# A decoder trunk on one core: the values are projected before the index queries, and four smaller moves go with it

## The chip, the core and the metric

The kernel runs on one core of a Trainium2 chip. The metric is the device time of one execution in microseconds (us). The core has TensorE for matrix products (PE in the profile, with its weight loads as PEld), VectorE (DVE), ScalarE (ACT), GpSimd (POOL) and SyncE (SP), which here only issues DMAs. DMAs are issued from the queues of SP, ACT and POOL.

## The reference, cut to what matters

The trunk is one layer with 512 tokens and 2048 channels. Everything is float32. What the change touches:

```python
mod = silu(c) @ w_ada + b_ada                     # six rows of 2048: sh1, sc1, gt1, sh2, sc2, gt2
h = rmsnorm(x, g_mix) * (1 + sc1) + sh1
proj = h @ w_in                                   # q_a k_a v_a q_b k_b v_b qi ki wi g_a g_b
y_a = stick_breaking_attention(q_a, k_a, v_a) @ w_a
y_b = dsa_attention(rope(q_b), rope(k_b), v_b, rope(qi), rope(ki), wi) @ w_b
x = x + (1 + gt1) * ((sigmoid(g_a) * y_a + sigmoid(g_b) * y_b) @ w_o)
h = rmsnorm(x, g_ffn) * (1 + sc2) + sh2
u = h @ w_up;  u = conv_b + width-3 causal convolution of u over tokens
x = x + (1 + gt2) * ((silu(u[:, :5632]) * u[:, 5632:]) @ w_down)
return rmsnorm(x, g_final)
```

`qi` are the 1024 columns of the index queries, `v_a` the 1024 columns of the stick-breaking values. A fact that both versions use: with `amp = (1 + sc1) * g_mix` and `r = 1/rms(x)` of a token, `h @ w = r * ((x * amp) @ w) + sh1 @ w`. So a projection can start on `h0 = x * amp` before the norm is known; the product is then scaled by `r`, and a row `sh1 @ w`, the same for every token, is added. That row is called the shift row below.

## The kernel before

**Products.** Each float32 product is made of three fast ones: an operand is split into a high part (`hi`, `wh`: ACT copies it to a shorter format) and a low part (`lo`, `wl`: DVE subtracts), and `mm3` (L178 to L180) adds hi*hi, hi*lo and lo*hi in PSUM. `prep` loads a 128x1024 tile of weights (`raw`, 8 buffers, loaded by SP) and `parts` (L168 on ACT, L170 on DVE) splits it into one of three pairs of rooms `wh`, `wl`. PSUM has eight banks: `acc` (3), `att` (4), `outs` (1).

**adaLN.** `mod` is made on DVE: `ada_half` (L320, L321) loads 512 KB of `w_ada` and one DVE instruction multiplies it by a spread copy of `silu(c)` and sums it. There are two spread copies, `cb[0]` and `cb[1]`, for the first and the second 1024 channels, and each stays in a `raw` buffer, so that six are left for loads. 96 such halves (`ada_left`) are spread over later stages by `some_ada`.

**Stage 1, index queries (L396 to L427).** For each of the 16 tiles of 128 channels: two adaLN halves give `sc1` of the tile, `h0` is formed, and seven of the eight index query tiles are accumulated in seven PSUM banks. After the last tile the norm (`rms`, L368 to L379) is spread to all partitions.

**Stage 2, values (L459 to L480).** `h` is formed (L437 on DVE, L438 and L466 on ACT, L468 on DVE), its shift `sh1` by two more adaLN halves per tile, and the eight value tiles are accumulated in eight banks. Then come the small `tail` product, the eighth index query tile (`w_qi7`) and the first two query and key tiles.

**Stage 3, 31 units (L675 to L685).** `unit` makes two output tiles with one Strassen step: seven products of 8x3 matmuls of 128x256, whose weights DVE adds and subtracts (L268, L272, L306, L310) before they are split. At two places of each unit `between` takes one step of a list of tasks (`beside`): `rope_tables`, `shift_queries`, `index_ropes`, and then adaLN halves. `shift_queries` reads `w_qi` transposed and makes the shift row of the index queries by 28 DVE instructions; `index_ropes` scales a query tile by the norm (L647), adds the shift (L648, ACT) and rotates it (L616 to L624). At the second place a unit also makes one adaLN half.

**Stage 4, attention and output projection.** For each of 8 stick-breaking heads and 8 sparse heads DVE makes adaLN halves beside the attention, two per head in the first loop and four in the second; the indexer's top-128 search (MAX8, MATCH_REPLACE8, L779 and L780) runs on DVE beside the sticks.

**Stage 5, up-projection.** Six up tiles (`ups`, NU = 3 pairs) are made plainly while the second norm is applied; they stay in SBUF and are convolved by `finish` (L1123 to L1133) beside the first three units of the up-projection (j = 3, 4, 5), each of which also finishes its own pair. `yd` takes the results.

The order on each engine is that of the program as a scheduling layer arranges it from the code's order and `issue_after` pins (`behind`). The engines take their queues in order.

Of the kernel before, what the change touches and what calls it, by code (L numbers as in the profile page):

```python
# [35 lines left out]
NQ = 7  # L36
# [40 lines left out]
def block_kernel(ctx: ExitStack, tc: tile.TileContext, A: dict, out: bass.AP):  # L77
# [279 lines left out]
    cb = c_spread()  # L357
    nc.scalar.dma_start(c_col, A["c_col"])
# [3 lines left out]
    def rms(squares, blocks=range(NQB), bank=outs):  # L362
# [14 lines left out]
        yield  # L377
        out = bank()
        mm(out[:, at], ones, wide[:, at], start=True, stop=True)  # L379
# [4 lines left out]
    qi_ps = [acc() for _ in range(3)] + [att() for _ in range(4)]  # L384
    norm = None
# [10 lines left out]

    for k in range(KT):
        if k == 6:
            past = t2k("w", 2)[:, :P]
            with behind(pins["load"]):  # L400
                nc.sync.dma_start(const, A["consts"][:, :5])
                nc.sync.dma_start(past, A["consts"][:, 5])
            nc.gpsimd.tensor_copy(mask[0], ident)
            nc.gpsimd.tensor_copy(mask[1], past)
# [6 lines left out]
        if k == KT - 1:  # L411
            norm = rms([total])
            next(norm)
        ada_end(t, t + 1)
        stt(amp[:, 0, k : k + 1], mod[:, t : t + 1], 1.0, g_mix[:, k : k + 1], ALU.add, ALU.mult)
        h0 = slot(F32R), slot(F32R)
        act(h0[0], x, AF.Copy, scale=amp[:, 0, k : k + 1])
        stt(h0[1], x, amp[:, 0, k : k + 1], h0[0].bitcast(F32), ALU.mult, ALU.subtract)  # L418
        w = prep(A["w_qi"][k], NQ * P)
        for j in range(NQ):  # L420
            mm3(qi_ps[j], cols(w, j), h0, k == 0, k == KT - 1)
            if k == KT - 1 and j == 0:
                rstd = t2k("T", 2)
                act(rstd, next(norm), AF.Copy)
# [3 lines left out]


    dram = lambda name, n, w=S: [dr.tile([P, w], F32, tag=f"{name}{i}", name=f"{name}{i}") for i in range(n)]  # L430
    save = nc.gpsimd.dma_start
    qid, hd_, vd, rd = dram("qid", 8), dram("hd", KT // 2), dram("vd", 8), dram("rd", 1)[0]
    save(rd, rstd)
# [8 lines left out]
    def evac(ps, rows=slice(0, P)):  # L442
        o = slot()
        act(o[rows], ps[rows], AF.Copy)
        return o

    EARLY = (9,)
# [7 lines left out]
    pv = None  # L455

    def ada_tile(k):
        last = [ada_half(cb, k, half) for half in range(2)][1]
        ada_end(k, k + 1)  # L459
        return last  # L460

    ada_tile(0)
    for k in range(KT):
        modulate(xt[k], k, 0, xt[k])
        hi, lo = slot(F32R), slot(F32R)
        act(hi, xt[k], AF.Copy)  # L466
        with behind(*([ada_tile(k + 1)] if k + 1 < KT else [])):
            tt(lo, xt[k], hi.bitcast(F32), ALU.subtract)  # L468
        h.append((hi, lo))
        w = prep(A["w_va"][k])  # L470
        if k == 0:
            for j in range(NQ):
                save(qid[j], evac(qi_ps[j]))
            pv = [outs()] + [acc() for _ in range(3)] + [att() for _ in range(4)]
        if k % 2 == 0:
            save(hd_[k // 2], xt[k])
        for i in range(8):
            mm3(pv[i], cols(h[k], i % 4), cols(w, i // 4, S), k == 0, k == KT - 1)
        if k in EARLY:
            forms_late(EARLY.index(k))  # L480
    for i in range(8):
        save(vd[i], evac(pv[i]))
# [15 lines left out]
    for j, (src, dst) in enumerate(((A["w_qi7"], qid[7]), (A["w_x0"][0], xd[0]), (A["w_x0"][1], xd[1]))):  # L498
        ps = (acc, att)[j % 2]()
        for c in range(2):  # L500
            w = prep(src[c])
            for k in range(8):
                i = 8 * c + k
                last = mm3(ps, cols(w, k), h[i], i == 0, i == KT - 1)
                if j == 2 and k % 2:
# [81 lines left out]
    corr = macc[:, : 2 * NQ, :].rearrange("p (j a) b -> p j (a b)", a=2)  # L587

    def shift_queries():

        rows = [t2k(tag, 2) for tag in ("w", "T") for _ in range(2)]
        diag = None
        for i in range(5):
            if i:
                ps = outs()
                mm(ps, ones, diag, start=True, stop=True)
                act(rows[i - 1], ps, AF.Copy)
            if i < 4:
# [1020 lines left out]
```

## Time and profile before

| what | value |
|---|---|
| median of 3 runs | 2746.66 us (2745.15 to 2747.31) |
| the profiled execution's own time | 2744.77 us |
| its span, first to last instruction | 2742.9 us |
| busy: PE, DVE, ACT, POOL | 98%, 88%, 53%, 11% of the span |
| stage 1 (first product to the spread norm) | 13.5 to 98 us |
| stage 2, with the tail and the small tiles | 101.6 to some 239 us |
| stage 3 | some 239 to 830 us |
| attention | some 865 to 1180 us |
| first units of the up-projection | some 1500 to 1560 us |

In a row of a timeline stand the start, the busy time, engine, line, operation, out<-in and shape, and in brackets the idle time in front and what ended it. In a row of windows stand for each engine the busy time in the stretch and the number of instructions, the granted clock of PE, the share of the DMA engines and GB/s. A busy PE is modelled, so beside its busy time the number of matmuls is used: it shows what was really done in a stretch.

### The profile page before, as it was taken

What the parts mean: (1) busy time and instruction counts of PE and PEld (TensorE: products, weight loads), DVE (VectorE), ACT (ScalarE), POOL (GpSimd) and SP (SyncE); (2) the same over time, 40 slices, a digit from 0 to 9 for tenths busy, and PEclk for the clock granted to TensorE, in tenths of its full rate; (3) what the DMA queues carried; (4) which work ended last, traced back from release to release, by engine and by line L of the source; (5) the groups of instructions that cost most, each with busy time, mean ns of one, the idle gap of its engine ahead of it and who ended that gap; (6) DMA issues with size and microseconds to landing.
All of it is one profiled execution on the core that took longest, in us unless ns stands there. A gap on an engine that the chain in (4) does not pass through costs nothing. (4 is left out here: it accounts for less than half of the span.)

```text
span 2742.9 us, 47708 instructions
## 1 busy us (share of the span) xinstructions
PE 2678.6 (98%) x18704; PEld 2449.0 (89%) x18704; DVE 2409.0 (88%) x3452; ACT 1450.6 (53%) x2045; POOL 314.2 (11%) x519
## 2 busy tenths in 40 slices
PE   8999999999999999999999999999999999999996
PEld 6779999999998777889999999999999998888875
DVE  8978989988897899788888999999999997888876
ACT  4444454455556665434466555555555455546452
POOL 0010000001002011111220100000000001012112
PEclk9999999999999999999999999999999999999998
DMA  9973456755566458866773566666665436559686
GB/s 339 363 258 123 163 177 207 234 178 185 173 209 222 137 190 279 270 222 190 229 254 114 173 185 177 182 181 178 183 177 166 137 123 234 169 158 257 192 243 188
DMA packets 164189, 550.08 MB, mean 201 GB/s; under 512 B 21414, under 2 KB 21798, under 8 KB 163964
## 3 DMA queue, kind: packets, MB, share of 16 engines
q1 hardware_dynamic: 116220, 405.34, 44.7%
q0 software_dynamic: 47152, 141.30, 18.4%
q8 instruction: 147, 2.41, 0.3%
q14 instruction: 78, 0.64, 0.1%
q10 hardware_dynamic: 592, 0.39, 0.0%
HBM read 453.71 MB, written 89.83 MB: 198 GB/s over the span
## 5 line engine op out<-in xcount | busy, mean ns | idle before, releaser
L168 ACT ACTIVATE wh<-raw 128x1024 fp32r<-128x1024 f32 (+2 forms) x792 | 828.1, 1053 | 942.4 <-DVE raw L272 180.0
L170 DVE TENSOR_TENSOR wl<-raw,wh 128x1024 fp32r<-128x1024 f32 (+2 forms) x792 | 953.3, 1211 | 123.4 <-ACT wh L168 115.4
L178 PE MATMUL acc<-F,wh 128*128 128x256 f32 (+1 forms) x2464 | 706.9, 289 | 15.2 <-ACT wh L168 10.7
L180 PE MATMUL acc<-F,wl 128*128 128x256 f32 (+1 forms) x2464 | 706.8, 287 | 5.4 <-DVE wl L170 5.4
L179 PE MATMUL acc<-F,wh 128*128 128x256 f32 (+1 forms) x2464 | 707.4, 287 | 0.0
L178 PE MATMUL att<-F,wh 128*128 128x256 f32 (+1 forms) x2448 | 700.1, 288 | 5.2 <-DVE sp L308 4.2
L180 PE MATMUL att<-F,wl 128*128 128x256 f32 (+1 forms) x2448 | 700.5, 286 | 2.1 <-DVE wl L170 2.1
L179 PE MATMUL att<-F,wh 128*128 128x256 f32 (+1 forms) x2448 | 701.1, 286 | 1.2 <-DVE F L199 1.2
L178 PEld LDWEIGHTS acc<-F,wh 128*128 128x128 f32 x2464 | 462.4, 188 | 33.0 <-ACT wh L168 15.2
L180 PEld LDWEIGHTS acc<-F,wl 128*128 128x128 f32 x2464 | 462.7, 188 | 16.4 <-DVE wl L170 6.8
L178 PEld LDWEIGHTS att<-F,wh 128*128 128x128 f32 x2448 | 459.7, 188 | 18.0 <-issue 5.6
L179 PEld LDWEIGHTS acc<-F,wh 128*128 128x128 f32 x2464 | 463.1, 188 | 11.0 <-DVE F L418 0.9
L179 PEld LDWEIGHTS att<-F,wh 128*128 128x128 f32 x2448 | 459.7, 188 | 12.7 <-DVE F L199 4.3
L180 PEld LDWEIGHTS att<-F,wl 128*128 128x128 f32 x2448 | 459.6, 188 | 11.0 <-DVE wl L170 2.9
L321 DVE SCALAR_TENSOR_TENSOR raw<-raw,raw 128x1024 f32<-128x1024 f32 x155 | 185.7, 1218 | 0.0
L178 PE MATMUL att<-wh,F 128*128 128x512 f32 x448 | 178.3, 398 | 0.2 <-ACT wh L168 0.2
L179 PE MATMUL att<-wl,F 128*128 128x512 f32 x448 | 174.8, 390 | 0.0
L180 PE MATMUL att<-wh,F 128*128 128x512 f32 x448 | 174.8, 391 | 0.0
L268 DVE TENSOR_TENSOR raw<-raw,raw 128x1024 f32<-128x1024 f32 x80 | 97.5, 1218 | 39.6 <-DMA raw<-in_w_x 22.3
L179 PE MATMUL acc<-wl,F 128*128 128x512 f32 x288 | 113.8, 395 | 4.4 <-DVE wl L170 4.4
L178 PE MATMUL acc<-wh,F 128*128 128x512 f32 x288 | 112.5, 393 | 1.1 <-ACT wh L168 0.9
L180 PE MATMUL acc<-wh,F 128*128 128x512 f32 x288 | 112.8, 392 | 0.0
(360 smaller groups left out, 3620.7 us busy)
## 6 DMA issues: line engine op xcount, KB each, us to landing
raw<-in_w_up SPq DMA_DIRECT2D x164, 512.0 KB, 3.6
raw<-in_w_ada SPq DMA_DIRECT2D x155, 512.0 KB, 5.4
raw<-in_w_x SPq DMA_DIRECT2D x128, 512.0 KB, 4.3
raw<-in_w_down SPq DMA_DIRECT2D x104, 512.0 KB, 5.0
xd<-F POOLq DMA_DIRECT2D x64, 256.0 KB, 2.8
F<-xd POOLq DMA_DIRECT2D x64, 256.0 KB, 5.0
raw<-in_w_o SPq DMA_DIRECT2D x32, 512.0 KB, 5.3
soft<-in_w_gate SPq DMA_DIRECT2D x32, 512.0 KB, 4.1
```

The costliest lines, as they stand in the source:

```text
L168: pins["wh"] = act(wh, raw, AF.Copy)
L170: pins["wl"] = tt(wl, raw, wh.bitcast(F32), ALU.subtract)
L178: mm(ps, ah, bh, start=first, stop=False, skip_group_check=not check)
L179: mm(ps, ah, bl, start=False, stop=False, skip_group_check=not check)
L180: return mm(ps, al, bh, start=False, stop=last, skip_group_check=not check)
L268: last_v = tt(s, a21, a22, ALU.add)
L321: return stt(raw, raw, 1.0, cb[half], ALU.mult, ALU.mult, accum_out=macc[:, t, half : half + 1])
```

## The change

Five things are done.

1. **Values first.** Stage 1 now accumulates the eight value tiles from `h0`; the last two of the 16 tiles are reordered around the norm, so that four value tiles are still being summed behind the product that spreads the norm. Stage 2 accumulates all eight index query tiles (NQ = 8) from the finished `h`, so `w_qi7`, the scaling by the norm and the saved norm row `rd` go. The value tiles are scaled by `r` on their way out of PSUM (ACT) and saved beside stage 2.
2. **The values' shift row** `sh1 @ w_va` is made by `shift_values`: POOL loads `w_va` again, ACT scales it by `sh1` per partition, POOL adds up (`gpsimd.tensor_tensor`), two matmuls with ones sum over partitions, and eight accumulating DMAs add the row to the saved values. `shift_queries` goes. The order of tasks is now rope tables, a pause of two steps, index ropes, `shift_values`.
3. **adaLN by first halves.** `ada_left` takes all first halves, then all second halves. So `cb[1]` is given up after stage 2 (a copy waits in DRAM, `c_half`) and comes back when the second halves start; until then seven `raw` buffers serve loads. From the start of `shift_values` on each unit makes two adaLN halves instead of one, and heads 5 to 7 of the first attention loop and parts of heads 0 and 1 of the second make none.
4. **Index ropes** fetch the next tile one step ahead.
5. **Plain up tiles late.** `ups` are saved to DRAM, and `finish_first` fetches and finishes them in 21 single steps, one in each unit from j = 9 on.

```diff
-    qi_ps = [acc() for _ in range(3)] + [att() for _ in range(4)]
+    pv = [outs()] + [acc() for _ in range(3)] + [att() for _ in range(4)]
...
-        w = prep(A["w_qi"][k], NQ * P)
-        for j in range(NQ):
-            mm3(qi_ps[j], cols(w, j), h0, k == 0, k == KT - 1)
+        wv.append(prep(A["w_va"][k]))
+        if k < KT - 2:
+            for i in range(8):
+                value(i, k)
...
+    ada_tile(0)
+    for i in range(1, 4):
+        value(i, KT - 2)
+    for k in range(KT - 2, KT):
+        value(0, k)
+    v0 = evac(pv[0])
+    norm = rms([total])
+    r_col = next(norm)
+    for i in range(4, 8):
+        value(i, KT - 2)
+    w_next = prep(A["w_qi"][0])
+    for i in range(1, 4):
+        value(i, KT - 1)
+    spread = next(norm)
+    act(rstd, spread, AF.Copy)
+    with behind(pins["spread"]):
+        for i in range(4, 8):
+            value(i, KT - 1)
...
-    def shift_queries():
...
+    def shift_values():
+        total = [t2k("T", 2) for _ in range(2)]
+        def weights(k):
+            w = sb.tile([P, 1024], F32, tag="soft", name=nm("soft"))
+            save(w, A["w_va"][k])
+            return [w[:, i * S : (i + 1) * S] for i in range(2)]
+        w = weights(0)
+        light.append(1)
+        yield
+        for k in range(KT):
+            for i in range(2):
+                act(w[i] if k else total[i], w[i], AF.Copy, scale=mod[:, k : k + 1])
+                if k:
+                    nc.gpsimd.tensor_tensor(total[i], total[i], w[i], ALU.add)
+            if k + 1 < KT:
+                w = weights(k + 1)
+            yield
...
-    ada_left = [(t, half) for t in range(32, 80) for half in range(2)]
+    ada_left = [(t, half) for half in range(2) for t in range(32, 80)]
+    cb[1] = None
...
-                if i:
+                if i or light:
                     some_ada()
...
-            some_ada(2)
+            some_ada(2 if hd < 5 else 0)
...
-            some_ada(2)
+            some_ada(2 if hd > 1 else 0)
...
-            some_ada(2)
+            some_ada(2 if hd else 0)
...
-    ups = [evac(ps) for ps in ups]
+    ud = dram("ud", 2 * NU)
+    for i, ps in enumerate(ups):
+        save(ud[i], evac(ps))
...
-        if j < 2 * NU:
-            finish(j - NU, *ups[2 * (j - NU) : 2 * (j - NU) + 2])
-        elif j < 2 * NU + 2:
+        if 2 * NU <= j < 2 * NU + 2:
...
+        if j >= 3 * NU:
+            run(first_tiles)
         finish(j, *unit(A["w_up"][j - NU], f, beside_up))
```

How the order of instructions moves at the places that matter. First PE at the border of stages 1 and 2. Before, L379 spreads the norm; of the last tile two products follow it, and then the first value product (`outs<-wh,F`), which needs the finished `h`:

```order
L180 MATMUL att_109<-F_771,wl_70 128x512
L178 MATMUL att_110<-F_771,wh_67 128x512
L379 MATMUL outs_783<-T_764,const 128x512
L179 MATMUL att_110<-F_772,wh_67 128x512
L180 MATMUL att_110<-F_771,wl_70 128x512
L178 MATMUL outs_876<-wh_73,F_840 128x512
```

Between the sums of squares (L368) and L379 stood 19 products. In the changed kernel L370 sums the squares and L381 spreads the norm:

```order
L180 MATMUL acc_108<-wh_67,F_779 128x512
L370 MATMUL outs_810<-const,T_122 128x1 x4
L178 MATMUL acc_109<-wh_67,F_778 128x512
L179 MATMUL acc_109<-wl_70,F_778 128x512
L180 MATMUL acc_109<-wh_67,F_779 128x512
L381 MATMUL outs_849<-T_818,const 128x512
L178 MATMUL att_110<-wh_67,F_778 128x512
```

Three products stand between the two now, and twelve (`att_110` to `att_113`) between L381 and the first product that needs `h`.

Second DVE in a unit of stage 3, from L310 to L268, the sum of two loaded tiles of the next unit. Before, in a unit with a step of `index_ropes` (L647):

```order
L170 TENSOR_TENSOR wl_70<-raw_7486,wh_67 128x1024
L170 TENSOR_TENSOR wl_76<-raw_7456,wh_73 128x1024
L310 TENSOR_TENSOR raw_7456<-raw_7456,raw_7486 128x1024
L170 TENSOR_TENSOR wl_83<-raw_7450,wh_79 128x1024
L276 TENSOR_TENSOR sp_7548<-att_7448,ta_7484 128x256
L647 TENSOR_TENSOR w_7518<-w_7518,w_5773 128x512
L321 SCALAR_TENSOR_TENSOR raw_7581,macc_68<-raw_7581,raw_92 128x1024
L170 TENSOR_TENSOR wl_70<-raw_7456,wh_67 128x1024
L268 TENSOR_TENSOR raw_7711<-raw_7677,raw_7679 128x1024
```

With six buffers the tile `raw_7679`, the second input of L268, takes the room of `raw_7450`, which the fourth row (`wl_83`) reads last. Now, in a unit beside `shift_values`:

```order
L310 TENSOR_TENSOR raw_6554<-raw_6554,raw_6584 128x1024
L170 TENSOR_TENSOR wl_83<-raw_6548,wh_79 128x1024
L276 TENSOR_TENSOR sp_6649<-att_6546,ta_6582 128x256
L321 SCALAR_TENSOR_TENSOR raw_6686,macc_68<-raw_6686,raw_92 128x1024
L170 TENSOR_TENSOR wl_70<-raw_6554,wh_67 128x1024
L268 TENSOR_TENSOR raw_6816<-raw_6782,raw_6784 128x1024
L170 TENSOR_TENSOR wl_76<-raw_6552,wh_73 128x1024
L308 TENSOR_TENSOR sp_6649<-att_6546,ta_6582 128x256
L321 SCALAR_TENSOR_TENSOR raw_6851,macc_68<-raw_6851,raw_92 128x1024
```

No task has a DVE instruction here any more, the unit has two adaLN halves (L321), and the later of the two loads waits for the room of `raw_6584`, which L310 reads last: four instructions ahead of L268, where in units beside the index ropes more stand between.

Third POOL in the same units. Before, its queue held only DMAs there. Now (L728 saves a unit's results, L623 loads `w_va`):

```order
L623 DMA soft_6220<-in_w_va 128x1024
L728 DMA xd_1771<-F_6215 128x512
L728 DMA xd_1772<-F_6216 128x512
L633 ISA
L633 TENSOR_TENSOR T_6153<-T_6153,soft_6220 128x512
L633 TENSOR_TENSOR T_6154<-T_6154,soft_6220 128x512
L623 DMA soft_6385<-in_w_va 128x1024
L633 TENSOR_TENSOR T_6153<-T_6153,soft_6385 128x512
L633 TENSOR_TENSOR T_6154<-T_6154,soft_6385 128x512
L623 DMA soft_6452<-in_w_va 128x1024
```

Each load stands behind the two additions that free its one room, and each pair of additions behind the two ACT instructions that scale what was loaded.

More of the change, by code (lines that the diff above doesn't have):

```diff
@@ L376, in rms @@
             ts(wide[:, b * P : (b + 1) * P], ident, r[:, b : b + 1], None, ALU.mult)
-        yield
+        yield r
         out = bank()
-        mm(out[:, at], ones, wide[:, at], start=True, stop=True)
+        pins["spread"] = mm(out[:, at], ones, wide[:, at], start=True, stop=True)
         yield out
     xt, total = [], None
-    qi_ps = [acc() for _ in range(3)] + [att() for _ in range(4)]
-    norm = None
+    pv = [outs()] + [acc() for _ in range(3)] + [att() for _ in range(4)]
     def next_x():
@@ L395, in next_x, with ada_tile, evac, value @@
         return total or sq
+    def ada_tile(k):
+        last = [ada_half(cb, k, half) for half in range(2)][1]
+        ada_end(k, k + 1)
+        return last
+    def evac(ps, rows=slice(0, P), scale=None):
+        o = slot()
+        act(o[rows], ps[rows], AF.Copy, **({} if scale is None else {"scale": scale}))
+        return o
+    h0, wv = [], []
+    def value(i, k):
+        mm3(pv[i], cols(h0[k], i % 4), cols(wv[k], i // 4, S), k == 0, k == KT - 1)
     for k in range(KT):
         if k == 6:
-            past = t2k("w", 2)[:, :P]
             with behind(pins["load"]):
[L401 to L404, printed above, removed]
+                nc.sync.dma_start(const[:, :2], A["consts"][:, :2])
         t = KT + k
@@ L440, in modulate @@
         return h
[L442 to L447, printed above, removed]
+    EARLY = (9, 13)
     h = []
@@ L586, in block_kernel @@
     rope_d = dram("rope", 2, 2 * S)
[L587 to L613 removed]
+    light = []
+    def shift_values():
[15 more added lines that the diff above has]
+            yield
+        for i in range(2):
+            ps = outs()
+            mm(ps, ones, total[i], start=True, stop=True)
+            act(total[i], ps, AF.Copy)
+            for b in range(NQB):
+                if b % 2 == 0:
+                    yield
+                save(vd[4 * i + b], total[i], accum_op=ALU.add)
     def rope_steps(src, dst, cosv, sinv, half, n, a, b):
@@ L661, in some_ada, with pause @@
             if ada_left:
+                if ada_left[0][1] and cb[1] is None:
+                    cb[1] = t2k("raw", 8, w=1024)
+                    nc.sync.dma_start(cb[1], c_half.to_broadcast([P, 1024]))
                 ada_half(cb, *ada_left.pop(0), tag)
+    def pause():
+        for _ in range(2):
+            some_ada(1, ("soft", 1))
+            yield
+    shift = shift_values()
     def beside():
-        for task in (rope_tables(), shift_queries(), index_ropes()):
+        for task in (rope_tables(), pause(), index_ropes(), shift):
             yield from task
@@ L685, in block_kernel @@
             save(xd[2 * u + i], o)
+    for _ in shift:
+        pass
     def fetch(src, rows=slice(0, P)):
```

133 lines of the change are left out of this document (70 added, 63 removed).

## The prediction

> **What bounds the kernel.** I read the page's totals first, then the trace in stretches, then the timelines of the stretches in which PE does less than it can.
>
> ```profile
> span 2742.9 us, 47708 instructions
> PE 2678.6 (98%) x18704; PEld 2449.0 (89%) x18704; DVE 2409.0 (88%) x3452; ACT 1450.6 (53%) x2045; POOL 314.2 (11%) x519
> ```
>
> PE is the bound of the whole, with DVE close behind. So only stretches where PE waits can give anything. The stretches that the change touches, and three calm ones to measure them by (the x after PE is the number of matmuls):
>
> ```profile
> 13.50:97.50 84.00, 81.77 (x345) 64.69 (x345) 80.50 (x149) 34.70 (x47) 0.59 (x2) 1.00 0.94 346
> 97.50:113.00 15.50, 12.39 (x41) 9.15 (x40) 14.91 (x26) 12.21 (x19) 5.51 (x10) 0.78 0.97 361
> 125.00:225.00 100.00, 100.00 (x442) 80.74 (x442) 80.14 (x143) 46.29 (x64) 8.15 (x15) 1.00 0.69 243
> ...
> 385.00:545.00 160.00, 159.82 (x1386) 157.72 (x1386) 148.42 (x214) 68.44 (x85) 9.75 (x18) 1.00 0.65 214
> 545.00:725.00 180.00, 175.98 (x1540) 175.03 (x1539) 159.50 (x194) 102.65 (x137) 16.25 (x30) 1.00 0.56 180
> 725.00:800.00 75.00, 75.00 (x663) 75.00 (x662) 68.45 (x83) 45.82 (x62) 8.14 (x15) 1.00 0.59 190
> 800.00:815.00 15.00, 12.31 (x94) 12.11 (x94) 11.90 (x15) 5.36 (x9) 2.15 (x4) 0.89 0.69 217
> 1020.00:1040.00 20.00, 16.98 (x66) 10.35 (x65) 20.00 (x45) 13.67 (x27) 0.61 (x1) 1.00 0.18 54
> 1040.00:1130.00 90.00, 90.00 (x476) 74.64 (x475) 87.75 (x188) 47.92 (x103) 17.84 (x33) 1.00 0.90 310
> 1505.00:1560.00 55.00, 52.05 (x439) 50.34 (x438) 52.10 (x65) 33.86 (x46) 4.91 (x8) 1.00 0.50 163
> 1700.00:1800.00 100.00, 100.00 (x885) 100.00 (x884) 94.00 (x112) 57.29 (x75) 7.08 (x10) 1.00 0.64 178
> ```
>
> Calm, PE does a 128x512 product in 100/442 = 0.226 us and a 128x256 one in 100/885 = 0.113 us; a unit of 7x8x3 takes 19.0 us. What is lost then follows from the counts. Stage 1 has 16x7x3 = 336 products, 76.0 us, in 84: 8.0 lost, with a slow start and the sums of squares in it; the waits in it are priced below. The border of stages 1 and 2 does 41 products, 9.3 us, in 15.5: 6.2 lost. 545 to 725 does 1540 instead of 1593: 6.0 lost. 800 to 815: 94 instead of 133, 4.4 lost. 1505 to 1560: 439 instead of 487, 5.4 lost. 1020 to 1040 is idle for 3.0, and DVE is full. 725 to 800 loses nothing. All in all some 30 us lie within reach.
>
> **Values first.** The number of products in both stages with the eighth query tile is the same, 16x8x3 twice. Only where they stand changes: 48 products (10.9 us) move from behind stage 2 into stage 1.
>
> ```profile
> 37.86 0.22 DVE L335 SCALAR_TENSOR_TENSOR mod<-macc,vec 128x1 f32<-128x1 f32 x1
> 38.23 1.09 DVE L170 TENSOR_TENSOR wl<-raw,wh 128x896 fp32r<-128x896 f32 x1
> 42.91 0.22 DVE L335 SCALAR_TENSOR_TENSOR mod<-macc,vec 128x1 f32<-128x1 f32 x1
> ```
>
> A tile of stage 1 takes DVE 42.91 - 37.86 = 5.05 us against 21 x 0.226 = 4.75 us on PE, so DVE sets the pace and PE loses 15 x 0.30 = 4.5 us. A full 128x1024 low part takes 0.13 us more (1.22, below, against 1.09): 5.18 us on DVE, but 24 x 0.226 = 5.43 us on PE. PE becomes the bound of stage 1, and the waits shrink to those on DMA, which stands at 0.94: of 4.5 us I keep 2, and 0.4 is lost by a larger first tile. That is -2.1.
>
> At the border the chain from the spread norm to the first product is this:
>
> ```profile
> 97.03 1.02 PE L379 MATMUL outs<-T,const 128*128 128x512 f32 x2
> 97.49 0.80 PE L179 MATMUL att<-F,wh 128*128 128x512 f32 x1
> ...
> 98.09 0.60 ACT L424 ACTIVATE T<-outs 128x512 f32<-128x512 f32 x1 [4.82 <-PE outs L379]
> 98.58 1.05 ACT L168 ACTIVATE wh<-raw 128x1024 fp32r<-128x1024 f32 x1
> 99.53 1.54 ACT L438 ACTIVATE F<-w,mod,amp 128x512 f32<-128x512 f32 x2
> 100.97 0.61 ACT L466 ACTIVATE F<-F 128x512 fp32r<-128x512 f32 x1
> 98.79 0.69 DVE L437 TENSOR_TENSOR w<-F,T 128x512 f32<-128x512 f32 x1 [0.59 <-ACT T L424]
> 101.64 0.80 PE L178 MATMUL outs<-wh,F 128*128 128x512 f32 x1 [3.11 <-ACT F L466]
> ```
>
> PE waits 3.11 us and then runs slower (0.78 of the clock granted in that stretch). In the new order L168 and one of the two L438 leave the chain, 0.60 + 0.69 + 0.77 + 0.61 and the handovers, about 3.0 us, behind which twelve products (2.7 us) stand. New waits come: only three products (0.7 us) cover the chain root, reciprocal and four diagonals in front of the spread (some 1.7 us), so 1.0; and the low part of `h` stands behind one more L437 and one L321 on DVE, so about 1.2. That makes 2.5 instead of 6.2: -3.7. If the pieces add up worse, or PE's clock drops again, nothing is gained here (0 to -6.2). The scaling by `r` is in the copies from PSUM that were there anyway (L444, now L405); at the 0.60 us of L424 they are faster than PE, which needs 3 x 0.226 = 0.68 us for each bank.
>
> **Index ropes and the free buffer.**
>
> ```profile
> 712.48 0.42 DVE L276 TENSOR_TENSOR sp<-att,ta 128x256 f32<-128x256 f32 x1
> 712.82 0.68 DVE L647 TENSOR_TENSOR w<-w,w 128x512 f32<-128x512 f32 x1
> 713.42 1.22 DVE L321 SCALAR_TENSOR_TENSOR raw<-raw,raw 128x1024 f32<-128x1024 f32 x1
> 714.56 1.22 DVE L170 TENSOR_TENSOR wl<-raw,wh 128x1024 fp32r<-128x1024 f32 x1
> 718.96 1.23 DVE L268 TENSOR_TENSOR raw<-raw,raw 128x1024 f32<-128x1024 f32 x1 [3.17 <-DMA raw<-in_w_x]
> 807.62 1.22 DVE L321 SCALAR_TENSOR_TENSOR soft<-soft,raw 128x1024 f32<-128x1024 f32 x1 [2.02 <-DMA soft<-in_w_ada]
> ```
>
> The loss at 545 to 725 is this wait: L268 needs a tile whose load could start only when an older tile's last reader was done. Start to start these rows take 0.34, 0.60, 1.14 and 1.14 us; by the order only some 3.2 us of DVE work lie between that reader and L268, and the load takes about as long. With seven buffers some 6.1 us of DVE work lie there beside the index ropes, so the wait goes. That such a cover suffices is seen at 385 to 545, where some 4.9 us lay in between and 1386 products and four matmuls with ones (0.46 us each, as L379) fill 160 us but for about 1.6. The L647 scaling goes too. I take -5 of 6.0 (0 to -6). The wait at 807.62 is for the one `soft` room, just left by the last index rope; the adaLN halves that use it come two steps or more after its last other use now: -4 of 4.4. Two of these four matmuls also go: -0.9.
>
> **The shift row by ACT and POOL, and two adaLN halves per unit.** This is what may cost. In such a unit DVE has 13 operations at 1.14 us and 5 at 0.34, 16.6 us of 19.0, so 2.4 are free, if POOL leaves it alone. POOL's 30 additions of 128x512 have no row in this trace. The nearest is a copy of 128x128 on POOL:
>
> ```profile
> 37.78 0.29 POOL L403 CAST mask<-const 128x128 bf16<-128x128 f32 x1 [37.33 <-DMA const<-in_consts]
> 43.58 0.30 POOL L404 CAST mask<-w 128x128 bf16<-128x128 f32 x1 [5.51 <-DMA w<-in_consts]
> 43.04 0.69 DVE L394 TENSOR_TENSOR T<-T,w 128x512 f32<-128x512 f32 x1
> 43.64 0.25 DVE L415 SCALAR_TENSOR_TENSOR amp<-mod,vec 128x1 f32<-128x1 f32 x1
> 49.08 0.68 DVE L394 TENSOR_TENSOR T<-T,w 128x512 f32<-128x512 f32 x1
> 49.68 0.15 DVE L415 SCALAR_TENSOR_TENSOR amp<-mod,vec 128x1 f32<-128x1 f32 x1
> ```
>
> By it an addition takes between 0.3 and 4 x 0.29 = 1.16 us. The last four rows show a DVE instruction in the same place twice: beside the copy it takes 0.25 us and ends with it (43.89), alone 0.15. One case, but it speaks for DVE waiting while POOL reads. (The first copy delayed nothing: the L335 at 37.86 took its 0.22.) If each addition stops DVE for its whole length, a unit with four loses 4.6 us of DVE, 2.2 more than is free, in 7.5 units 17 us; and the loads, which start only after the additions, may then hold up ACT's queue, where the high parts stand behind the scaling, by 1 to 1.4 us a unit, 10 more. If DVE is not stopped, nothing to 3 us is lost: 3.7 us of DVE work cover a load now, against 3.2 in the stretch that lost 6.0 and 4.9 in the one that lost 1.6. Bounds 0 and +28. I take +10, for POOL will often run while DVE waits or reads PSUM. The Trainium skill, "SBUF — State Buffer", section "SBUF: two separate sides", says that DVE operations with two SBUF inputs and POOL operations that read SBUF hold one pair of ports exclusively for a whole instruction; the 0.25 us row agrees, the 0.22 us row does not show it. By the rule nearly each addition would stop DVE in full; what that gives is the first rival.
>
> On POOL the saves of results stand behind the additions; the results' rooms are 62 slots deep, so I cost that at nothing. If that cover is gone, the next unit's results wait for a slot, a few us in all. Accumulating into the saved values ends long before the sticks read them: nothing.
>
> **Attention.** By 1037 us heads 5 to 7 and the first sparse head drop some eight halves, 9 us of DVE work, where DVE is full and PE idles 3.0 us and is slowed by more: -4 (0 to -7). DVE stays full to 1130 with PE full too, so PE, once early, could wait there; four more halves less in that stretch cover it.
>
> **Up tiles late.** A `finish` is, start to start, four times 0.66 and 0.60 us:
>
> ```profile
> 1509.44 0.75 DVE L1125 SCALAR_TENSOR_TENSOR w<-F,cw,w 128x510 f32<-128x510 f32 x1
> 1510.10 1.22 DVE L170 TENSOR_TENSOR wl<-raw,wh 128x1024 fp32r<-128x1024 f32 x1
> 1511.24 0.69 DVE L1132 TENSOR_TENSOR w<-w,w 128x512 f32<-128x512 f32 x1
> 1511.84 1.22 DVE L170 TENSOR_TENSOR wl<-raw,wh 128x1024 fp32r<-128x1024 f32 x1
> ```
>
> 3.2 us, on top of a unit that already holds DVE at 0.94 of its 19.0 us (1700 to 1800): 1.1 free, so about 2.1 too much in each of three units, 6, which is the 5.4 lost. In single steps at most 0.66 us, once 1.3, comes on a unit: it fits. I take -4.5 (0 to -5.4); the six more saves and fetches are POOL's, which is busy for 7 of 100 us there.
>
> **The sum.** -2.1 - 3.7 - 5 - 4 - 0.9 - 4 - 4.5 = -24.2, and +10 for POOL: -14.2 on an execution of 2744.77 us (its span 2742.9 and 1.87 around it), 2730.6. The median of the runs, 2746.66, lies 1.89 above that execution, so 2732.5; I say 2732.
>
> **The rivals.** First, POOL stops DVE in full. Then the light units take 21.2 us or, with ACT held up, 22.6 instead of 19.0, which is +17 to +28: 2739.5 to 2750.5. For it speaks the 0.25 us row, and that nearly all DVE operations there have two SBUF inputs; against it, that DVE waits for PE in part of the unit. From 22.2 us a unit (24.2/7.5 = 3.2 more) on, the gains are eaten. Second, on the other side, the loads: POOL's additions, drawn out, delay the next 512 KB, ACT waits for it at the head of its queue, and DVE then for the next high part. L268's wait of 3.17 us shows what one load just missed costs DVE. With one such a unit on top of 21.2 it is 24 us, +37: 2759, slower. Against it speaks that a unit of 19 us holds only two such loads. Third, POOL costs nothing worth naming (+2): 2724.5; for it speaks the 0.22 us row. Fourth, the covers fail: the border keeps its 6.2 us since PE's clock drops again, and the attention's gain is taken by the wait for the search behind it. Then 24.2 shrinks to 16.5, with +10: 2740. That the values are not first or the halves not in this order can't be; the order shows both.
>
> **Chances.** The forecast, POOL at 5 to 15: 0.45, on its own 2726 to 2738. POOL in full, 2739 to 2751: 0.15; the loads in turn, slower: 0.10. POOL free: 0.20. Covers fail: 0.10. A measurement of this kernel tells about 0.2% (5.5 us) from no change, so faster is under 2741.2 and slower above 2752.2. Faster: 0.45 + 0.20 + 0.05 + 0.04 = 0.74; slower: 0.10 + 0.02 = 0.12; the rest 0.14. The range leaves out a tenth on each side: 2719, POOL free and every cover good, to 2752.
>
> **What would show it.** In the trace after: stage 1 with an L335 every 5.4 us and PE at 0.226 us per product; at the border waits of 1 us or less and the clock at 1.00; no L268 wait of 3 us beside the index ropes; no wait for `soft`; DVE operations of more than 1.3 us beside POOL's additions, and units of 19.0 to 20.5 us there; 1020 to 1040 without idle PE; the units of j = 3 to 5 at 19.0 us. I am wrong if units beside the additions take over 22 us, or if PE waits in new places at stage 3.

## The result, and the profile after

The changed kernel takes 2771.4 us (median of 4 runs, 2769.9 to 2773.8), the kernel before 2746.8 us beside it (2745.2 to 2747.3). The ratio is 1.0092 with a 95% interval of 1.0080 to 1.0104: slower by some 25 us. The forecast was 2732 us, the range ended at 2752, and the chance given to slower was 0.12. The profiled execution of the changed kernel has a span of 2769.7 us, 26.8 more than before. Its totals:

```profile
span 2769.7 us, 47729 instructions
PE 2687.6 (97%) x18700; PEld 2462.7 (89%) x18700; DVE 2412.6 (87%) x3369; ACT 1465.7 (53%) x2067; POOL 392.3 (14%) x584
```

They say little: DVE is as busy as before, POOL by 78 us more. Where the time went is found with one mark per unit. L306 runs once in every unit, and a unit without losses takes 19.0 us. The starts of the L306 rows, counted from the first unit of stage 3, cut both traces into the same pieces of work:

| piece | before, us | after, us | difference |
|---|---|---|---|
| start to unit 0 (stages 1 and 2) | 235.5 | 229.4 | -6.1 |
| 17 units, 0 to 16 | 334.2 | 330.5 | -3.7 |
| 13 units, 17 to 29 (from the start of the shift row on) | 257.0 | 287.4 | +30.4 |
| unit 30 and the attention | 419.9 | 413.3 | -6.6 |
| output projection, norm, plain up tiles | 238.2 | 237.2 | -1.0 |
| first 4 units of the up-projection | 85.2 | 79.9 | -5.3 |
| next 21 units | 400.0 | 421.9 | +21.9 |
| next 15 units | 290.4 | 290.4 | 0 |
| the rest | 482.6 | 479.7 | -2.9 |

So the gains came: the pieces that fell add up to 25.6 us. Of these the -1.0 and the -2.9 are not the change's to claim, for across all the kernels traced here these two pieces took 235.4 to 238.9 and 478.3 to 483.1 us, with the code of the last one the same in all. Two pieces took 52 us. The windows of the changed kernel show the same (columns as before; the x after PE counts matmuls):

```profile
13.50:92.00 78.50, 78.46 (x336) 64.28 (x335) 76.57 (x136) 34.79 (x45) 0.41 (x1) 1.00 0.98 359
92.00:112.00 20.00, 18.81 (x83) 14.40 (x82) 12.88 (x27) 11.49 (x18) 4.91 (x9) 1.00 0.69 236
400.00:560.00 160.00, 160.00 (x1414) 160.00 (x1413) 148.98 (x179) 91.64 (x119) 17.84 (x33) 1.00 0.61 192
600.00:760.00 160.00, 143.24 (x1187) 141.72 (x1186) 141.05 (x141) 81.38 (x112) 66.33 (x57) 0.96 0.65 208
...
1028.00:1048.00 20.00, 19.65 (x83) 14.40 (x82) 20.00 (x46) 15.30 (x26) 0.00 (x0) 1.00 0.10 27
1515.00:1560.00 45.00, 45.00 (x399) 45.00 (x398) 41.83 (x50) 27.64 (x36) 2.51 (x4) 1.00 0.57 169
1600.00:1980.00 380.00, 367.46 (x3165) 365.74 (x3164) 344.69 (x412) 211.46 (x271) 32.13 (x47) 0.98 0.65 177
```

400 to 560, beside the index ropes, is full: 1414 matmuls in 160 us. 600 to 760, the light units beside the shift row, does 1187; the 227 missing are 25.7 us at 0.113. There the granted clock is 0.96. Beside the late up tiles, 1600 to 1980, some 200 are missing.

**A light unit.** The timeline of one, all engines (most PE rows and all weight loads left out):

```profile
636.48 0.41 DVE L308 TENSOR_TENSOR sp<-att,ta 128x256 f32<-128x256 f32 x1
...
637.33 1.34 ACT L631 ACTIVATE soft<-soft,mod 128x512 f32<-128x512 f32 x2 [4.22 <-DMA soft<-in_w_va]
...
638.13 3.50 POOL L633 TENSOR_TENSOR T<-T,soft 128x512 f32<-128x512 f32 x2 [5.22 <-ACT soft L631]
...
638.57 1.99 ACT L168 ACTIVATE wh<-raw 128x1024 fp32r<-128x1024 f32 x2
...
639.27 1.25 DVE L321 SCALAR_TENSOR_TENSOR raw<-raw,raw 128x1024 f32<-128x1024 f32 x1 [2.38 <-DMA raw<-in_w_ada]
...
639.98 0.28 PE L179 MATMUL acc<-F,wh 128*128 128x256 f32 x1
...
640.45 1.47 DVE L309 TENSOR_TENSOR F<-sp,ta 128x256 f32<-128x256 f32 x1
...
641.84 1.21 DVE L170 TENSOR_TENSOR wl<-raw,wh 128x1024 fp32r<-128x1024 f32 x1
...
643.11 0.52 PE L180 MATMUL acc<-F,wl 128*128 128x256 f32 x1 [2.85 <-DVE wl L170]
```

The load that L321 waits for, from SP's own timeline:

```profile
634.31 2.60 SPq L320 DMA_DIRECT2D raw<-in_w_ada  x2
```

Three things are to be read here. L321, the second adaLN half, waits 2.38 us for its load, the first of the two that SP issues from 634.31 on, so 5.0 us after its issue (the other load is for a later half). ACT stands 4.22 us at L631 for the one `soft` room, with the high parts (L168) behind it. And L309, which takes 0.42 us elsewhere, takes 1.47 beside the two additions. PE waits 2.85 us for the low part that comes out of this chain. The waits of DVE in all light units, in us in total, times and longest:

```profile
DVE raw L321 <- DMA raw<-in_w_ada: 25.4, 11, 4.7
DVE wl L170 <- ACT wh L168: 2.8, 7, 1.1
```

The view of DVE's waits charges the loss to one load. The experiments show that this is less than half of it.

**A unit with a late up tile** (ACT and DVE rows near PE's wait; POOL's fetch from its own timeline, in the fence behind):

```profile
1616.32 1.22 DVE L306 TENSOR_TENSOR raw<-raw,raw 128x1024 f32<-128x1024 f32 x1
...
1617.85 0.82 ACT L1289 ACTIVATE T<-F,cw 128x512 f32<-128x512 f32 x1 [4.79 <-DMA F<-ud]
...
1618.57 1.04 ACT L168 ACTIVATE wh<-raw 128x1024 fp32r<-128x1024 f32 x1
...
1620.35 0.75 DVE L1170 SCALAR_TENSOR_TENSOR w<-F,cw,w 128x511 f32<-128x511 f32 x1 [2.82 <-ACT w L1169]
```

```profile
1608.69 0.87 POOL L1267 DMA_DIRECT2D gates<-soft  x1 [4.36 <-ACT soft L1266]
1609.26 0.87 POOL L736 DMA_DIRECT2D F<-ud  x1
```

L1289 is the first step on a fetched tile. ACT stands at it for 4.79 us, a high part waits behind it, and DVE waits 2.82 us. The fetch was issued at 1609.26 and ACT went on at 1617.85, 8.6 us later. There are six fetches, and ACT waits 26.8 us for them in all.

### The profile page after: what moved, and what is told of

Read it like the earlier page. It is cut to its first block, busy times and chain, and to the rows that moved or that the text cites. A ratio compares the mean times of both kernels' runs of the same rounds, so it can differ in the third digit from the quotient of the medians.

```text
span 2769.7 us, 47729 instructions
## 1 busy us (share of the span) xinstructions
PE 2687.6 (97%) x18700; PEld 2462.7 (89%) x18700; DVE 2412.6 (87%) x3369; ACT 1465.7 (53%) x2067; POOL 392.3 (14%) x584
## 4 chain that ended last, share of the span: by engine, by line
PE 79%; DVE 9%; DMA 6%; issue 4%; ACT 2%; POOL 0%; SPq 0%; DVEq 0%; ACTq 0%; POOLq 0%
PE att L180 12%; PE att L178 12%; PE att L179 12%; PE acc L180 11%; PE acc L179 11%; PE acc L178 11%; DVE wl L170 3%; DMA raw<-in_w_ada 2%; DMA F<-ud 1%; PE acc L892 1%; DMA raw<-in_w_down 1%; PE outs L179 1%; ACT wh L168 1%; PE outs L178 1%; PE outs L180 1%
## 5 line engine op out<-in xcount | busy, mean ns | idle before, releaser
L168 ACT ACTIVATE wh<-raw 128x1024 fp32r<-128x1024 f32 (+1 forms) x790 | 827.8, 1055 | 890.3 <-DVE raw L272 165.2
L170 DVE TENSOR_TENSOR wl<-raw,wh 128x1024 fp32r<-128x1024 f32 (+1 forms) x790 | 962.1, 1224 | 129.0 <-ACT wh L168 120.3
L180 PEld LDWEIGHTS acc<-F,wl 128*128 128x128 f32 x2448 | 461.7, 189 | 25.4 <-DVE wl L170 16.8
L321 DVE SCALAR_TENSOR_TENSOR raw<-raw,raw 128x1024 f32<-128x1024 f32 x152 | 189.3, 1266 | 28.1 <-DMA raw<-in_w_ada 28.1
L178 PEld LDWEIGHTS att<-wh,F 128*128 128x128 f32 x448 | 84.2, 188 | 20.1 <-issue 2.0
```

Source lines behind the costliest of these rows:

```text
L168: pins["wh"] = act(wh, raw, AF.Copy)
L170: pins["wl"] = tt(wl, raw, wh.bitcast(F32), ALU.subtract)
L178: mm(ps, ah, bh, start=first, stop=False, skip_group_check=not check)
L180: return mm(ps, al, bh, start=False, stop=last, skip_group_check=not check)
L321: return stt(raw, raw, 1.0, cb[half], ALU.mult, ALU.mult, accum_out=macc[:, t, half : half + 1])
```

## The experiments

Each time is a median with the ratio to the kernel before and its interval. In these comparisons the kernel before took 2746.5 to 2747.7 us. "Light units" means the 13 units of the table: 257.0 us before, 287.4 after, 247 without any loss. Two kernels below whose code is the changed kernel's in these units, the first and the fifth, took 284.4 and 285.2 there, so a difference of 3 us in them says little.

**1. The fetches by SP.**

```diff
-            u = fetch(ud[2 * j])
+            u = sp_fetch(ud[2 * j])
```

(`sp_fetch` issues `nc.sync.dma_start` into a slot; the second tile of a pair is fetched likewise)

> The changed kernel, but the six saved plain up tiles are fetched by SP's queue instead of POOL's. Theory A: in the changed kernel six units of the up-projection take 21.2 to 23.9 us instead of 19.0 because POOL issues the fetch only after its wait at L1267, and ACT then stands 4 to 5 us at L1289 in front of a high part. Then all units from the third fetch-free one on are 19.0 us again, the waits of L1289 vanish, and the time falls by 22 us, from 2771.4 to about 2749. Theory B: the single steps are too much DVE work for a unit: nothing changes, 2771. Theory C: SP's queue brings the fetch just as late, behind the weight loads: 2765 to 2771.

2766.2 us, 1.0070 (1.0051 to 1.0088). The 21 units still take 420.2 us, and ACT still waits 26.6 us. The fetch leaves at the same point of the unit, 7.1 to 7.2 us ahead of L306 in both kernels, and lands no earlier: ACT goes on 7.9 to 9.0 us after the issue, against 7.8 to 8.9 in the changed kernel. (The last row holds the two landings, of six, that the trace has.)

```profile
1603.21 0.33 SPq L1287 DMA_DIRECT2D F<-ud  x1
1611.54 0.82 ACT L1294 ACTIVATE T<-F,cw 128x512 f32<-128x512 f32 x1 [4.49 <-DMA F<-ud]
DMA to landing us min/median/max: 7.9/8.0/8.1
```

Theory A falls as it was put, and C holds: the queue is not what makes the tile late. Of the 5 us by which this kernel is faster than the changed one only 1.7 lie in the 21 units. In the order of the instructions ACT's step stands only four ACT rows behind L1266, for which POOL's fetch waits. The code asks for the tile one whole unit ahead, but the scheduling layer had moved the ACT step up by that unit, right behind the place of its fetch. That led to the fifth experiment.

**2. Both adaLN halves at the unit's second place.**

```diff
-                if i or light:
-                    some_ada()
+                if i:
+                    some_ada(2 if light else 1)
```

> The changed kernel, but the second adaLN half of a light unit is made at the unit's second place, beside the first one, where at least 3.7 us of DVE work stand between the release of a load's room and its reader instead of 2.6. DVE's and POOL's work are the same. Theory L: the wait of 2.3 us for this half's load is all of the loss, POOL's stalls (0.78 us for each addition) find free time on DVE: light units 19.0 us, 2771.4 - 38 = 2733. Theory P: POOL's stalls are the loss and the wait for the load only shows it: units stay at 22 to 23 us, 2768 to 2771. Theory S, both add up: 16.6 us of DVE work and 3.1 us of stalls are 19.7 us a unit, so about 12 x 2.6 = 31 us come back: 2740.

2757.1 us, 1.0037 (1.0023 to 1.0050); light units 276.3 us. No L321 waits any more, yet only 11 us of the 40 came back. None of the three theories gives this. A third wait took over: ACT's for the `soft` room (33.4 us in seven waits, 23.9 in the changed kernel), and DVE's for the high parts behind it.

```profile
DVE wl L170 <- ACT wh L168: 20.6, 18, 4.2
ACT soft L631 <- DMA soft<-in_w_va: 33.4, 7, 7.4
```

**3. No additions on POOL.**

```diff
                 act(w[i] if k else total[i], w[i], AF.Copy, scale=mod[:, k : k + 1])
-                if k:
-                    nc.gpsimd.tensor_tensor(total[i], total[i], w[i], ALU.add)
```

> The changed kernel without POOL's 30 additions: the shift row then holds only the first of its 16 terms, so a part of the computation is left out; loads, ACT's scaling and both adaLN halves stay. Theory L (the load of the second half): the wait of L321 stays at 2.3 us, units 21 to 22.5 us, 2755 to 2766. Theory P (POOL's stalls): light units 19.0 us, 2733. Theory S: 16.6 us of DVE work and a wait of up to 2.3 us are 18.9 us, so units of 19.0 to 19.5 us, 2733 to 2739.

2745.2 us, 0.9993 (0.9982 to 1.0004); light units 263.0 us. The 30 additions cost 26 us, 0.87 each. The time lies in none of the three ranges: the additions are not all (Theory P), nor the load (Theory L), and the sum of S was too low. What is left, 16 us above 247, stands beside two load waits: L321's for the second half's load, 31.6 us in twelve waits, and ACT's at L631 for the `soft` room, 20.7 us in seven. Only part of them reaches PE, and this run does not tell the two apart.

**4. The late up tiles alone, on the kernel before.**

```diff
-    ups = [evac(ps) for ps in ups]
+    ud = dram("ud", 2 * NU)
+    for i, ps in enumerate(ups):
+        save(ud[i], evac(ps))
...
+        if j >= 3 * NU:
+            run(first_tiles)
```

(with the rest of this part of the change)

> The kernel before with one part of the change alone, the plain up tiles saved, fetched and finished late. Theory A (POOL's fetch comes late): the first units of the up-projection win 5 us, six later units lose 22 us, so 2746.8 + 17 = 2763.5. Theory B' (the late fetches are late only because of what the earlier parts of the change did): 2742.

2759.1 us, 1.0046 (1.0031 to 1.0062). The first four units fall to 79.9 us, the 21 rise to 422.2: as in the changed kernel. This part loses 12 to 17 us by itself (12.6 by the medians, 16.9 by these two pieces of the trace), without the rest of the change: theory A's side.

**5. ACT's first step held back.** One pin: the step may not stand ahead of the high part that the code has formed last.

```diff
-            act(t, u, AF.Identity, scale=cw[:, j, 2:3], bias=cw[:, j, 3:4])
+            with behind(pins["wh"]):
+                act(t, u, AF.Identity, scale=cw[:, j, 2:3], bias=cw[:, j, 3:4])
```

> The changed kernel, but ACT's first step on a fetched up tile is held behind the last high part of the unit; the fetch itself stays on POOL's queue. In the order of the changed kernel this step stands only four ACT instructions behind the one that POOL's fetch waits for, about 4 us, and a fetch lands 6.5 us after its issue (8.0 on SP's queue); held back, it stands fifteen behind it, some 14 us. Theory A', the step is issued too close to its fetch: the six units of 21.2 to 23.9 us become 19.0, 2771.4 - 22 = 2749. Theory B, the steps are too much for DVE in a unit: they stay, 2771. If the fetch were simply slow (over 14 us): 2760 to 2771.

2750.6 us, 1.0005 (0.9993 to 1.0016), 21 us under the changed kernel. The 21 units take 402.9 us, and ACT no longer waits at this step. The fetch itself is unchanged: it lands 7.7 to 9.4 us after its issue here, and the step stands 18.1 us behind it. (The 6.5 us of the expectation is the middle of a view that holds the six saves too; the six fetches of the changed kernel land after 7.8 to 8.9.) Theory A' is shown: the use stood too close behind its fetch. That DVE has room for the single steps is shown with it: 2.9 us are left above the 400.0 of before. The same stretch as above:

```profile
1600.00:1980.00 380.00, 378.38 (x3333) 377.79 (x3332) 361.84 (x432) 225.35 (x288) 33.07 (x49) 1.00 0.67 186
```

**6. Both load waits taken away, the additions kept.** The second experiment's edit, and `w_va` goes into two slots one step ahead:

```diff
-            w = sb.tile([P, 1024], F32, tag="soft", name=nm("soft"))
-            save(w, A["w_va"][k])
-            return [w[:, i * S : (i + 1) * S] for i in range(2)]
+            w = [slot() for _ in range(2)]
+            for i in range(2):
+                save(w[i], A["w_va"][k][:, i * S : (i + 1) * S])
+            return w
...
         for k in range(KT):
+            ahead = weights(k + 1) if k + 1 < KT else None
...
-            if k + 1 < KT:
-                w = weights(k + 1)
+            w = ahead
```

> The changed kernel with both adaLN halves of a light unit at its second place (as in the second experiment) and the w_va tiles loaded into two of the 62 slots one step ahead instead of into the one soft room. POOL's additions, ACT's scaling and DVE's work are the same. Theory S (DVE's work, POOL's stalls and the two load waits add up): both waits are gone, DVE has 16.6 + 3.1 = 19.7 us to do in a unit, so 2771.4 - 40 + 12 x 0.7 = 2740. Theory P (the additions cost what they cost, loads aside): as the second experiment, 2757. Theory L (loads alone): units 19.0 us, 2732.

2757.2 us, 1.0034 (1.0020 to 1.0049); light units 269.7 us. Neither load is waited for any more, and a full light unit takes 21.3 us. The additions stand bare (DVE, and POOL from its own timeline):

```profile
628.38 0.42 DVE L276 TENSOR_TENSOR sp<-att,ta 128x256 f32<-128x256 f32 x1 [0.46 <-PE att L180]
628.72 1.44 DVE L321 SCALAR_TENSOR_TENSOR raw<-raw,raw 128x1024 f32<-128x1024 f32 x1
...
630.09 2.31 DVE L321 SCALAR_TENSOR_TENSOR raw<-raw,raw 128x1024 f32<-128x1024 f32 x1
...
632.33 1.21 DVE L170 TENSOR_TENSOR wl<-raw,wh 128x1024 fp32r<-128x1024 f32 x1
633.47 2.32 DVE L268 TENSOR_TENSOR raw<-raw,raw 128x1024 f32<-128x1024 f32 x1
635.71 2.30 DVE L170 TENSOR_TENSOR wl<-raw,wh 128x1024 fp32r<-128x1024 f32 x1
637.93 0.41 DVE L308 TENSOR_TENSOR sp<-att,ta 128x256 f32<-128x256 f32 x1
```

```profile
627.62 3.69 POOL L635 TENSOR_TENSOR T<-T,F 128x512 f32<-128x512 f32 x2 [3.67 <-ACT F L633]
633.06 3.87 POOL L635 TENSOR_TENSOR T<-T,F 128x512 f32<-128x512 f32 x2 [0.71 <-ACT F L633]
```

Four DVE operations of 1.21 to 1.22 us take 1.44, 2.31, 2.32 and 2.30: 3.5 us of stall in a unit. With 16.6 us of work DVE is taken for 20.1, and 1.2 more go in waits at fixed places, such as the 0.46 us for a product. The time is the one that theory P gave. Theory S had the stalls nearly right (3.1 us) and forgot that DVE cannot fill every gap; of the 2.4 us that the sum left free, half go in such waits. The two causes, the additions and the load waits, add up: 22.7 us above 247 here and 16.0 in the third experiment, together 38.7, against 40.4 in the changed kernel.

**7. One adaLN half per unit, loads one step ahead, additions kept.**

```diff
-                if i or light:
+                if i:
...
-            some_ada(2 if hd < 5 else 0)
+            some_ada(2)
```

(likewise `some_ada(2)` at the two places of the second attention loop, and the sixth experiment's loads)

> The changed kernel with one adaLN half per unit instead of two (the halves then stand beside the attention heads again, as before the change) and the w_va tiles loaded into slots one step ahead. POOL's additions stay. Theory S: DVE has 15.5 + 3.1 = 18.6 us in a unit of 19.0, units 19.0 to 19.3; the attention takes back its 4: 2771.4 - 40 + 2 + 4 = 2737. Theory P (POOL stops PE's unit whatever DVE has free): units 20.5 to 22, 2750 to 2765.

2741.6 us, 0.9980 (0.9971 to 0.9989); light units 251.8 us, most of them 19.4. The attention takes back 6.1 us (419.4 against 413.3). The stalls are still there, 22.3 us in all by the same reckoning that gives 23.5 in the changed kernel (in the next section), but with room on DVE they cost little: 4.8 us above 247. So theory P falls: POOL does not stop PE whatever DVE has free.

**8. The seventh and the fifth together.**

> The seventh and the fifth experiment together. If both theories (S and A') hold: 2737 - 22 = 2715, faster than both kernels. If only one of the two holds: 2737 to 2749.

2723.6 us, 0.9910 (0.9895 to 0.9924). Both causes hold side by side: 18 us under the seventh, and faster than both kernels. The 2715 is missed by 9 us, since the seventh came out 5 above its forecast and the pin gave 18 instead of 22.

**9. The changed kernel, its sum on DVE.**

```diff
-                act(w[i] if k else total[i], w[i], AF.Copy, scale=mod[:, k : k + 1])
                 if k:
-                    nc.gpsimd.tensor_tensor(total[i], total[i], w[i], ALU.add)
+                    stt(total[i], w[i], mod[:, k : k + 1], total[i], ALU.mult, ALU.add)
+                else:
+                    act(total[i], w[i], AF.Copy, scale=mod[:, k : k + 1])
```

> The changed kernel, but scaling and adding up of the shift row is one DVE instruction per half tile (30 of some 0.60 us, start to start) instead of ACT's scaling and POOL's addition. Loads and adaLN halves stay. If an addition on POOL costs DVE 0.78 us of stall (23.5 us in all), the same sum costs DVE less when it does it itself (18 us): units of 20.5 to 22 us, 2752 to 2765. Rival, DVE is too full for work of its own and POOL took more off it than it cost: 2771 or more.

2747.9 us, 1.0003 (0.9992 to 1.0013), 23.5 us under the changed kernel; light units 263.6 us. The theory's side is right and its price too high: the sum on DVE takes only 2.7 us more than no sum at all (third experiment), which the two intervals do not tell from nothing, and 0.6 us more in the light units, though it is 30 instructions of 0.74 us (0.66 from start to start).

```profile
L632 DVE SCALAR_TENSOR_TENSOR T<-soft,mod,T x30: 737/743/754, 600.9 to 738.0; 128x512 f32<-128x512 f32 x30
DVE raw L321 <- DMA raw<-in_w_ada: 11.2, 5, 2.8
```

DVE does this work in part while it would have waited for the second half's load: L321 waits 11.2 us instead of 31.6. The edit also takes ACT's scaling away, and with it ACT's wait at its head for the `soft` room (DVE now waits for it, 2.2 us in all), so the 23.5 us are not those of the additions alone.

**10. The eighth with the sum on DVE.**

> The eighth experiment with the sum on DVE as in the ninth. DVE has 15.5 + 4 x 0.60 = 17.9 us to do in a unit instead of 15.5 + 3.5 = 19.0: units 19.0 instead of 19.4 to 20.1, 2723.6 - 5 = 2719. Rival: what DVE does itself comes at a worse place than the stalls: 2724 to 2735.

2719.5 us, 0.9902 (0.9887 to 0.9917), the lowest median of all, as forecast; but the interval overlaps the eighth's, so that the 4 us between the two are not shown. Its light units take 249.7 us, and 600 to 760 is full:

```profile
600.00:760.00 160.00, 160.00 (x1406) 159.42 (x1406) 151.02 (x180) 77.32 (x101) 25.39 (x45) 1.00 0.68 218
```

**11. Copies instead of additions.**

```diff
-                    nc.gpsimd.tensor_tensor(total[i], total[i], w[i], ALU.add)
+                    nc.gpsimd.tensor_copy(total[i], w[i])
```

> The changed kernel, but POOL copies the scaled tile into the sum's place instead of adding it, so the sum is left out; everything else stays. If any POOL operation that reads SBUF stops DVE operations with two SBUF inputs: stalls of 0.5 to 1.1 us for each copy, 2762 to 2771. If only POOL operations with two SBUF inputs do: no stalls, 2745 as without additions.

2752.3 us, 1.0020 (1.0010 to 1.0030); light units 270.3 us, between no additions (263.0) and additions (287.4). A copy has one SBUF input and still stops DVE:

```profile
649.17 1.62 DVE L170 TENSOR_TENSOR wl<-raw,wh 128x1024 fp32r<-128x1024 f32 x1
...
659.01 0.82 DVE L309 TENSOR_TENSOR F<-sp,ta 128x256 f32<-128x256 f32 x1
```

Each is 0.40 us over its calm time. In all, the DVE operations that overlap a copy take 7.3 us more than calm ones, as much as the light units take more than without additions. So one SBUF input on POOL is enough; the stall is shorter because the copy is. The prices that I had written (0.5 to 1.1 us, 2762 to 2771) were too high.

## Why the prediction was wrong, point by point

**Stage 1 and the border (-2.1, -3.7): the sum is right, its split by luck.** The first unit starts 6.1 us earlier against 5.8 forecast. 336 products took 84.0 us and take 78.5, so stage 1 gave more than its 2.1, in part because the sums of squares moved to the border. At the border 92 to 112 holds 83 matmuls, of which 73 are products, eight the sums of squares and two the spread of the norm, so 3.5 us are lost to products there and 1.2 more in 112 to 125 (52 products); counted the same way 6.7 were lost before, so the border gave 2.0 us and not 3.7. The wait in front of the spread was right (0.94 us, 1.0 forecast), and the clock stayed at 1.00. I looked for an L335 every 5.4 us; they come every 5.15, as DVE runs ahead while PE is full.

**Index ropes, `soft` wait, two matmuls (-5, -4, -0.9): right.** The units beside the index ropes take 19.0 us each; neither the L268 wait nor the `soft` wait of L321 appears there. (One `soft` wait of 2.84 us, at 386.52, stands ahead of them in the pause; I had expected none.) Units 0 to 29 lost 21.2 us before; after, the 17 ahead of the shift row lose 7.5.

**Attention (-4): right in kind, -6.6.** PE was busy for 16.98 of 20 us at 1020 to 1040 and is busy for 19.65 of 20 us at 1028 to 1048. The seventh experiment put the halves back and lost 6.1 us with them.

**Up tiles late (-4.5): the gain came, -5.3, and the cost was missed.** The failing step is the sentence that the six saves and fetches are POOL's, which has time. That POOL has time says nothing about when the tile lands, and I costed the new wait at ACT's head at nothing. It cost 21.9 us. That the steps themselves fit, which I also wrote, was right (fifth experiment). I had not looked up in the order where ACT's first step stands; it was there to be read, four ACT rows behind the one that releases the fetch.

**POOL's additions and the second half (+10, bounds 0 to +28): mis-sized, and the bounds too.** The light units came to +40 above 19.0 us each. Two steps failed.

- The price of an addition. From a 128x128 copy I bounded it by 0.3 and 1.16 us. The shortest of the 30 takes 1.29 us; the median is longer, since an addition waits for DVE too (row below: shortest, median and longest in ns). The DVE operations that overlap an addition took 23.5 us more than the median of the same operations without one, 0.78 us for each addition. That is 61% of 30 x 1.29, nearer to the first rival ("POOL stops DVE in full") than to my +10, which rested on POOL running "often" while DVE waits or reads PSUM. What I said of PSUM is right: L276, which reads a product from PSUM, takes 0.42 us inside an addition (628.38 in the sixth experiment) as elsewhere.

```profile
L633 POOL TENSOR_TENSOR T<-T,soft x30: 1287/1852/2266, 605.9 to 766.4; 128x512 f32<-128x512 f32 x30
```

- The load of the second adaLN half. I wrote that 3.7 us of DVE work cover a load now. For L268 that was enough (it waits 0.3 us once); for the L321 at the unit's first place only 2.6 us (L268, L170 and L308) stand between the release of its room and its use. It waits eleven times, 25.4 us in all, and then goes on 4.2 to 7.0 us after its load's issue. My own row had spoken against 3.7: at 718.96 L268 went on 6.4 us after its room was free, 3.2 of work and 3.17 of wait, so the load did not take "about as long" as the 3.2. And I counted 7.5 units, those with additions; the two halves stand in all 13, and 9.2 of the 40 us are lost in the five of them in which no addition runs. The second rival had the mechanism of a load that takes its turn, with ACT at its head, and it too is there (4.22 us at L631), but its price of a missed load was put in one rival and not into the sum.

The threshold was sound: I wrote that over 22.2 us a unit the gains are eaten, and nine of the units took 22.3 to 24.2. Each gain of the sum had a row behind it, while one cost was the middle of a guess and the other was nothing. The balance: I forecast a change of the span of -14.2 us and +26.8 was measured, 41 us apart. The light units cost 30 us more than I took (40 instead of 10) and the late tiles 22. Against that stand 11 us by which the gains exceeded my 24.2: they came to 35.6, with the 10 that the light units had lost before, and with the 3.9 that are not the change's.

The Trainium skill, "SBUF — State Buffer", section "SBUF: two separate sides", says that the one of the two engines that starts first holds the shared ports for its whole instruction while the other fully blocks. The traces agree in both directions: L309 takes 1.47 us instead of 0.42 behind an addition, and an addition that comes behind L321 (at 639.41) takes 2.23 instead of 1.29. By that rule the first rival would have been the forecast; it ended at 2750.5 us, still 21 short, for it held neither the second half's load nor the late tiles.

## What to carry to other kernels

Work given to POOL beside a full DVE isn't free: 30 additions cost DVE 23.5 us of stall and the kernel 26, while the same sum as DVE instructions, with ACT's scaling gone too, cost 2.7 by the medians, which their intervals do not tell from nothing. A wait for a load is priced at its tightest user, not at the one that waited last time; look up for each moved load how much work stands between the release of its room and its reader. And a fetch asked for "one step ahead" in the code is ahead only if the order shows it: where a scheduler may move the user up, pin the user.

## What the runs showed of the hardware that I had not expected

**A wait of PE costs more than its length.** After the wait of 2.85 us at 640 PE's granted clock is 0.50 for 3.4 us: 16 matmuls instead of 30, so 1.6 us more.

```profile
640.00:643.20 3.20, 0.35 (x4) 0.15 (x2) 3.20 (x5) 0.56 (x1) 2.21 (x2) 1.00 0.48 152
643.20:646.60 3.40, 3.40 (x16) 3.40 (x17) 3.37 (x5) 1.36 (x2) 0.55 (x1) 0.50 0.71 231
646.60:650.00 3.40, 3.40 (x32) 3.40 (x31) 3.19 (x4) 2.18 (x4) 0.55 (x1) 1.00 0.51 130
```

Of the ten waits of 1.8 to 2.1 us in the units of the changed kernel, six were followed by about 16 slow matmuls and four by none. That is why the units with a late tile took 21.2 and 21.7 us or 22.7 to 23.9, with nearly the same wait. The place of the wait decides. In the units every slow stretch lasts 3.41 us, and their starts lie whole multiples of that length apart (643.20, 667.10 and 711.47 us by 7 and by 13 of them), so the trace can be cut into frames of 3.41 us:

```profile
663.69:667.10 3.41, 1.43 (x13) 1.23 (x12) 3.41 (x4) 0.63 (x1) 1.45 (x2) 1.00 0.64 179
667.10:670.50 3.40, 3.40 (x19) 3.40 (x18) 3.37 (x5) 1.69 (x3) 0.55 (x1) 0.50 0.54 208
684.15:687.57 3.42, 2.88 (x26) 2.68 (x24) 3.12 (x3) 2.27 (x3) 3.35 (x2) 1.00 0.41 132
687.57:690.98 3.41, 2.00 (x17) 2.01 (x18) 3.38 (x5) 0.63 (x1) 1.12 (x2) 1.00 0.80 231
690.98:694.39 3.41, 3.41 (x32) 3.41 (x32) 3.35 (x5) 2.65 (x4) 0.55 (x1) 1.00 0.50 163
```

A wait of 1.98 us lies whole in the first frame, and the next runs at 0.50. A wait of 1.95 us is shared by the third and the fourth, and no slow one follows. In the units of this trace each of the nine slow frames comes behind one in which PE was idle for 1.76 us or more, and none behind one of 1.60 or less: the border is near half a frame; in the units of the other kernels the two cases overlap between 1.6 and 1.9 us. Five of the nine stand in the light units and four among the late tiles, 1.7 us each, so some 15 of the 52 us came this way. Without the additions (third experiment) none stands in the light units. The Trainium skill, "TensorE: Matmul & The Clock Gate", Part 1, puts the drop behind an idle window of some 3.4 us that runs freely. The trace agrees with a window that runs freely; that about half of it is enough does not fit a whole idle window, and here the measurement decides.

**A small fetch lands late among large ones.** 256 KB took 8.0 us on SP's queue (the two landings that the trace has), issued behind 512 KB loads of `w_up`, and 7.8 to 8.9 us in six fetches on POOL's queue. Whether the bytes ahead of it or the queue make the time was not tried.
